# Values of both attentions projected with tokens on the partitions, 512 columns at a time, in two steps over K that hold four PSUM banks

## The chip, the cores and the metric

The kernel runs on one core of a Trainium2 chip (trn2). The metric is the device time of one execution in microseconds (us). The engines are named as the profile names them: PE (TensorE, with its weight loads PEld), DVE (VectorE), ACT (ScalarE), POOL (GpSimd) and SP (SyncE, which here issues the DMAs).

## What is computed

A trunk of two layers over 1024 tokens of width 1024, in float32. Only the mixer of the first layer is touched:

```
proj = rms_norm(x) @ w_in
gq, gk, gv, gr, glr, sq, sk, sv = split(proj, [256, 256, 512, 512, 16, 512, 512])
o_gla = gla_mixer(gq, gk, gv, gr, glr, ...)        # 4 heads, chunks of 64, decayed state
o_sb  = stick_breaking_mixer(sq, sk, sv, ...)      # 8 heads of 64, causal, no softmax
mix   = concat([o_gla, o_sb]) @ w_out
```

The mixer is followed by a SwiGLU block, a convolution layer and a second SwiGLU block, which the change leaves alone. The values are `gv` (512 columns of `w_in`, from column 512) and `sv` (512 columns, from column 2576).

## The kernel before

Every product of float32 matrices is made from three matmuls: both operands are split into a high and a low part (`split`, L88: ACT writes the high part, DVE the difference), and `mm3` (L211, matmuls at L213, L214 and L215) adds high by high, high by low and low by high in one PSUM bank. The normed input stands transposed in SBUF as `hT[h]`, one half h of 512 tokens each, features on the partitions (`hh_a`, `hl_a` in the trace).

A projection is made by `project2` (L435) for 256 columns of the weight and one half of the tokens: the weight columns are the stationary operand, the 512 tokens move, and each chunk of 128 columns fills one bank of the PSUM tag "a" (2 banks). The other tags are "b" (2 banks), "zw" (3) and "o" (1). Tiles of split weights come from a pool of 8 (`ws`), of which a `project2` step holds 4; raw weights have 2 buffers.

- `sb_v` (L577 to L586) uses `project2`, so its result stands with features on the partitions. ACT copies it out (`vt`), PE transposes it in four pieces into a bank of tag "b" (`vp`, L582), DVE copies that out (`vo`, L584), and a DMA stores it.
- `gla_v` makes the token layout directly: 128 tokens are stationary and 256 weight columns move, into half a bank of tag "a" (`pm_gv`), 24 matmuls for each of 4 token tiles, and ACT copies it out.
- `sb_q` also makes the sums of squares of a chunk on PE into a bank of tag "b" (`ms_q`, L556), which DVE reads in the first instruction of the inverse root (`nv_q`, L106).
- `gla_gate` (L469) makes the decay: `pm_glr`, then four single float32 matmuls `pg` (L484) into tag "a", each emptied by DVE and ACT (`lm`, `la`).

`run` takes a list of steps, hand-ordered at the end of the function. Each step's weights are fetched one step ahead. Steps of attention (`a0` for the first half of the tokens, `a1` for the second), of the decayed state (`g0`, `g1`) and of its output (`o0`, `o1`) are wrapped in `first`, which gives them a high priority: the scheduler places them as early as their inputs allow, and the projections that stand near them in the list fill PE between them. A unit of attention runs from PE (`z`) to ACT (sigmoid), DVE (a scan and a multiplication, `b`), PE (transposes `wt`), ACT and DVE (split into `wth`, `wtl`), PE (`po`) and back to ACT and DVE (`og`). The order on each engine is fixed when the program is built; each engine runs its list in order and waits on semaphores.

Of the kernel before, what the change touches and what calls it, by code (L numbers as in the profile page):

```python
# [8 lines left out]
F32 = mybir.dt.float32  # L9
F32R = mybir.dt.float32r  # L10
# [8 lines left out]
P = 128  # L19
D = 1024  # L20
T = 1024
NK = D // P
# [14 lines left out]
def r32(ap):  # L37
    return ap.bitcast(F32)
# [3 lines left out]
def trunk(ctx, tc, x, mix_norm, ffn_norm, hy_w_in, hy_w_gate2, hy_b_gate, hy_gla_norm,  # L42
          hy_sb_q_norm, hy_sb_k_norm, hy_w_out, cv_w_pw1, cv_b_pw1, cv_w_dw, cv_b_dw,
          cv_ln_g, cv_ln_b, cv_w_pw2, cv_b_pw2, ffn_w_gate, ffn_w_up, ffn_w_down, out):
    nc = tc.nc
# [8 lines left out]
    ident = const.tile([P, P], F32, name="ident")  # L54
# [33 lines left out]
    def split(hi, lo, src, scale=None, eng=None):  # L88
        if scale is None:
            nc.scalar.copy(hi, src)  # L90
            (eng or nc.vector).tensor_sub(lo, src, r32(hi))  # L91
        else:
            nc.scalar.mul(hi, src, scale)
            nc.vector.scalar_tensor_tensor(lo, src, scale, r32(hi), op0=ALU.mult, op1=ALU.subtract)
# [3 lines left out]
    raw_p = weights_es.enter_context(tc.tile_pool(name="raw", bufs=2))  # L98
    ws_p = weights_es.enter_context(tc.tile_pool(name="ws", bufs=8))
# [59 lines left out]
    def load_cols(w, c0, name, n=256):  # L159

        raw = raw_p.tile([P, NK, n], F32, name=f"raw_{name}", tag="raw")
        nc.sync.dma_start(raw, w[:, c0:c0 + n].rearrange("(k p) c -> p k c", p=P))
        return raw
# [7 lines left out]
    def parts(raw_ap, name, shape=(P, NK, P)):  # L171
        hi = ws_p.tile(list(shape), F32R, name=f"wh_{name}", tag="ws")
        lo = ws_p.tile(list(shape), F32R, name=f"wl_{name}", tag="ws")
        split(hi, lo, raw_ap, eng=weight_engine[0])
        return hi, lo
# [16 lines left out]
    def run(steps):  # L192
        ready = [s for s in steps if isinstance(s, tuple)]
        got = {}

        def fetch():
            if ready:
                s = ready.pop(0)
                got[id(s)] = s[0]()

        fetch()
        for s in steps:
            if isinstance(s, tuple):
                w = got.pop(id(s))
                fetch()
                s[1](w)
                marks.append(next(i for i in reversed(nc.cur_bb.bb.instructions) if i.engine == DVE))
            else:
                s()

    def mm3(ps, sh, sl, mh, ml, first, last, **kw):  # L211

        nc.tensor.matmul(ps, sh, mh, start=first, stop=False, **kw)  # L213
        nc.tensor.matmul(ps, sh, ml, start=False, stop=False, **kw)  # L214
        nc.tensor.matmul(ps, sl, mh, start=False, stop=last, **kw)  # L215
# [25 lines left out]
    def sub(i):  # L241
        return slice(P * (i % 4), P * (i % 4) + P)
# [88 lines left out]
    w_in = hy_w_in[0]  # L331
# [4 lines left out]
    gv_d = dr("gv_d", [T, 512])  # L336
    q_d = dr("q_d", [4, P, T])
    k_d = dr("k_d", [4, P, T])
    v_d = dr("v_d", [4, P, NT, P])
# [30 lines left out]
    with ExitStack() as es:  # L370
# [7 lines left out]
        class Ps:  # L378
            BUFS = {"a": 2, "b": 2, "zw": 3, "o": 1}

            def tile(self, shape, dt, name, tag):
                return psp.tile(shape, dt, name=name, tag=tag, bufs=self.BUFS[tag])

        ps = Ps()
        psum = lambda tag, name: ps.tile([P, 512], F32, name, tag)
        ft = lambda name: ftp.tile([P, 512], F32, name=name, tag="ft")
# [39 lines left out]
        hT = []  # L426
# [8 lines left out]
        def project2(c0, name, h, consume):  # L435

            def weights():
                raw = load_cols(w_in, c0, f"{name}{h}")
                return [parts(raw[:, :, P * c:P * c + P], f"{name}{h}{c}") for c in range(2)]

            def body(ws):
                for c, w in enumerate(ws):
                    pm = psum("a", f"pm_{name}_{c}{h}")
                    for k in range(NK):
                        mm3(pm, w[0][:, k, :], w[1][:, k, :], hT[h][0][:, k, :], hT[h][1][:, k, :],
                            k == 0, k == NK - 1)
                    consume(c, pm)

            return weights, body
# [62 lines left out]
                nc.sync.dma_start(gq_d[:, c, hsl(h)], s)  # L512
            return project2(0, "gq", h, consume)

        def gla_v(c, h):
            def weights():
                raw = load_cols(w_in, 512 + 256 * c, f"gv{c}{h}")
                return [parts(raw[:, 4 * kk:4 * kk + 4, :], f"gv{c}{h}{kk}", (P, 4, 256)) for kk in range(2)]

            def body(ws):  # L520
                for i in range(4 * h, 4 * h + 4):
                    pm = psum("a", f"pm_gv{c}{i}")[:, 0:256]
                    hh, hl = hT[i // 4]
                    for k in range(NK):
                        wh, wl = ws[k // 4]
                        mm3(pm, hh[:, k, sub(i)], hl[:, k, sub(i)], wh[:, k % 4, :], wl[:, k % 4, :],
                            k == 0, k == NK - 1)
                    vt = ft(f"gv_{c}{i}")[:, 0:256]
                    nc.scalar.copy(vt, pm)
                    nc.sync.dma_start(gv_d[P * i:P * i + P, 256 * c:256 * c + 256], vt)  # L530

            return weights, body

        def gate_r(r, h):
            def consume(c, pm):
# [26 lines left out]
        def sb_k(p2, h):  # L562
            def consume(c, pm):
                sq = ft(f"sq_k{p2}{c}{h}")
                nc.scalar.activation(sq, pm, AF.Square)
                y = ft(f"y_k{p2}{c}{h}")
                nc.vector.tensor_scalar_mul(y, pm, gk)
                ms = psum("b", f"ms_k{p2}{c}{h}")
                nc.tensor.matmul(ms, hones, sq, start=True, stop=True)
                act_in_set(sq, ms, AF.Ln, bias=eps_t)  # L570
                act_in_set(sq, sq, AF.Exp, scale=-0.5)
                nc.vector.tensor_mul(y, y, sq)
                nc.sync.dma_start(k_d[2 * p2 + c, :, hsl(h)], y)
            return project2(2064 + 256 * p2, f"k{p2}", h, consume)

        def sb_v(p2, h):
            def consume(c, pm):  # L577
                vt = ft(f"vt{p2}{c}{h}")
                nc.scalar.copy(vt, pm)
                pt = psum("b", f"vp{p2}{c}{h}")  # L580
                for i in range(4):
                    nc.tensor.transpose(pt[:, i * P:(i + 1) * P], vt[:, i * P:(i + 1) * P], ident)  # L582
                vo = ft(f"vo{p2}{c}{h}")
                nc.vector.tensor_copy(vo, pt)  # L584
                nc.sync.dma_start(v_d[2 * p2 + c, :, 4 * h:4 * h + 4, :], vo.rearrange("p (i d) -> p i d", i=4))
            return project2(2576 + 256 * p2, f"v{p2}", h, consume)  # L586


        def sb_units(h):
# [227 lines left out]
        def first(f):  # L817
            def run_first():
                with tc.high_priority(2000):
# [3 lines left out]
        a0, a1, g0, g1, o0, o1 = [[first(s) for s in f(h)] for f in (sb_steps, gla_steps, gla_out_steps)  # L823
                                  for h in range(2)]
        w0 = out_project(0, ps, lambda name: bcp.tile([P, T], F32, name=name, tag="bc")[:, 0:512])
# [3 lines left out]
        use_ln_exp = lambda: load_set(LN_EXP_SET)  # L829
        use_sigmoid = lambda: load_set(SIGMOID_SET)  # L830
        lx0, lxa = (lambda: load_x(0)), (lambda: xa.append(load_xa(1)))
        norm1 = lambda: input_norm(1, input_stats(1))
        q, k, v, gv, r = [[[f(p2, h) for h in range(2)] for p2 in range(2)]
                          for f in (sb_q, lambda p2, h: sb_k(p2, h), sb_v, gla_v, gate_r)]
        gkk, gqq = [[f(h) for h in range(2)] for f in (gla_k, gla_q)]
        q00 = q[0][0]

        def first_weights():
            with tc.issue_after(first_mul[0]), tc.issue_after(first_mul[1]):
# [1 line left out]

        q[0][0] = (first_weights, q00[1])
        first_mul = list(last_mul)
        run([q[0][0], lxa, load_columns, k[0][0], norm1, q[1][0], k[1][0], (gate_weights, gla_gate), v[0][0],
             use_sigmoid] + a0[:2] + [v[1][0]] + a0[2:4] + [gkk[0]] + a0[4:6] + [gqq[0]] + a0[6:8] + [gv[0][0]]
            + a0[8:10] + [gv[1][0]] + g0[:1] + a0[10:12] + [r[0][0]] + g0[1:2] + a0[12:14] + [r[1][0]] + g0[2:3]
            + a0[14:] + [q[0][1]] + g0[3:] + [v[0][1]] + o0[:2] + [q[1][1]] + o0[2:] + [v[1][1], gkk[1], lx0]
            + w0[0:1] + [gqq[1]] + w0[1:3] + [use_ln_exp, k[0][1], k[1][1], use_sigmoid] + w0[3:4] + [gv[0][1]]
            + w0[4:] + [gv[1][1], r[0][1], r[1][1]]
            + a1[:2] + [ffn_in] + interleave(f0[:-12], interleave(a1[2:], g1 + o1)) + f0[-12:])  # L850


# [184 lines left out]
    hT = {}  # L1037
# [4 lines left out]
    with ExitStack() as es:  # L1042
# [7 lines left out]
        ft = lambda name: ftp.tile([P, 512], F32, name=name, tag="ft")  # L1050
# [145 lines left out]
        c0 = conv_steps(0, range(NK))  # L1196
# [9 lines left out]
        blocks, _ = token_sums(1, hT["f10"], ps, ("n", "a"), ft, xn)  # L1206
        run(f10[14:16] + f10[17:])

    with ExitStack() as es:
        weight_engine[0] = nc.vector  # L1210
        steps, late = five_products(1, blocks, es, (("act", 6), ("s", 4), ("ft", 10)))
        store = lambda j: [nc.sync.dma_start(xout[i * P:(i + 1) * P, 512 * j:512 * j + 512],
                                             xres[i][:, 512 * j:512 * j + 512]) for i in range(NT)]
# [25 lines left out]
```

## Time and profile before

| | |
|---|---|
| median of 3 runs | 2274.56 us (2270.47 to 2276.02) |
| profiled execution | 2270.5 us, span 2268.7 us, granted clock 0.997 |
| PE busy | 2233.4 us, 98% of the span |
| DVE busy | 1579.7 us, 70% |
| ACT busy | 956.7 us, 42% |
| POOL busy | 493.9 us, 22% |
| bytes moved by DMA | 247.98 MB, mean 109 GB/s |

A matmul's busy time in the timeline covers its way through the array and overlaps its neighbours; what one costs is the distance between the starts of two that follow each other. One float32 matmul that isn't split leaves two records.

### The profile page before, as it was taken

Reading aid. Unit: us, or ns where it says so; the run is one execution under the profiler, and the core shown is the slowest. Engines: PE = TensorE matmul, PEld = TensorE weight load, DVE = VectorE, ACT = ScalarE, POOL = GpSimd, SP = SyncE. Lnnn points to the kernel's source line nnn. Section 1 sums busy time; section 2 is a strip of 40 time slices with the busy share of each in tenths; the row PEclk is TensorE's granted clock in tenths of the full one; section 3 lists DMA queues with packets and bytes.
Section 4 is the critical chain, followed back from the end, with each engine's and each line's share of the span. In section 5 each row is a group of like instructions: output and inputs, shape, how many; then the busy total and the mean of one; then the engine's idle time right before and its main releaser. Section 6 shows DMA issues by size and latency. Waiting matters only on the chain.

```text
span 2268.7 us, 28065 instructions
## 1 busy us (share of the span) xinstructions
PE 2233.4 (98%) x10602; PEld 1849.0 (82%) x10602; DVE 1579.7 (70%) x2647; ACT 956.7 (42%) x1594; POOL 493.9 (22%) x273
## 2 busy tenths in 40 slices
PE   7999999999999999999999999999999999999999
PEld 6788888888888887888888888788888788888887
DVE  6587764867788755466767744498844887787786
ACT  6465644755555433422222244466454322222221
POOL 0000000000000002544444444787744300000000
PEclk9999999999999999999999999999999999999999
DMA  6254554333342333232223322223432322232222
GB/s 207 97 155 147 183 177 134 105 90 100 128 123 77 119 120 136 77 110 93 93 80 106 112 84 93 93 93 125 134 104 84 110 90 84 66 111 85 65 89 93
DMA packets 221749, 247.98 MB, mean 109 GB/s; under 512 B 9733, under 2 KB 171632, under 8 KB 221614
## 3 DMA queue, kind: packets, MB, share of 16 engines
q1 hardware_dynamic: 221614, 246.19, 33.6%
q8 instruction: 83, 1.36, 0.2%
q14 instruction: 52, 0.43, 0.1%
HBM read 219.42 MB, written 26.74 MB: 108 GB/s over the span
## 4 chain that ended last, share of the span: by engine, by line
PE 91%; DVE 5%; ACT 2%; DMA 1%; issue 1%; SPq 0%; DVEq 0%; ACTq 0%
PE po L213 9%; PE po L214 9%; PE po L215 9%; PE pu L213 5%; PE pu L215 5%; PE pu L214 5%; PE pg L213 4%; PE pg L215 4%; PE pg L214 4%; PE pp L213 2%; PE pp L214 2%; PE pp L215 2%; PE po L684 2%; PE wt L666 1%; PE ps3u L213 1%; PE ps3u L214 1%
## 5 line engine op out<-in xcount | busy, mean ns | idle before, releaser
L1131 DVE SCALAR_TENSOR_TENSOR cs<-u,wd,cs 128x512 f32<-128x512 f32 x406 | 306.0, 754 | 11.1
L237 DVE TENSOR_TENSOR xr<-xr,po 128x512 f32<-128x512 f32 x232 | 158.5, 684 | 156.7 <-PE po L215 155.7
L91 POOL TENSOR_TENSOR wl_wo<-raw_wo,wh_wo 128x1024 fp32r<-128x1024 f32 x8 | 19.1, 2395 | 882.0 <-ACT wh_wo L90 882.0
L1026 DVE TENSOR_TENSOR xr<-xr,po 128x512 f32<-128x512 f32 x176 | 120.0, 683 | 100.6 <-PE po L215 100.5
L213 PE MATMUL pg<-hh_f,wh_g 128*128 128x512 f32 x440 | 173.4, 394 | 3.8 <-DVE s L285 3.6
L213 PE MATMUL po<-wh_d,a 128*128 128x512 f32 x440 | 173.5, 395 | 0.2
L214 PE MATMUL pg<-hl_f,wh_g 128*128 128x512 f32 x440 | 173.4, 394 | 0.0
L215 PE MATMUL pg<-hh_f,wl_g 128*128 128x512 f32 x440 | 173.0, 393 | 0.0
L214 PE MATMUL pu<-hl_f,wh_u 128*128 128x512 f32 x440 | 172.7, 393 | 0.0
L215 PE MATMUL pu<-hh_f,wl_u 128*128 128x512 f32 x440 | 172.4, 392 | 0.0
L213 PE MATMUL pu<-hh_f,wh_u 128*128 128x512 f32 x440 | 172.3, 392 | 0.0
L215 PE MATMUL po<-wh_d,a 128*128 128x512 f32 x440 | 171.9, 391 | 0.0
L214 PE MATMUL po<-wl_d,a 128*128 128x512 f32 x440 | 171.9, 391 | 0.0
L90 ACT CAST wh_g<-raw_g 128x1024 fp32r<-128x1024 f32 x55 | 58.0, 1054 | 167.7 <-PE po L214 100.2
L90 ACT CAST wh_d<-raw_d 128x1024 fp32r<-128x1024 f32 (+1 forms) x58 | 58.4, 1008 | 113.4 <-PE pu L214 62.2
L91 POOL TENSOR_TENSOR wl_g<-raw_g,wh_g 128x1024 fp32r<-128x1024 f32 x33 | 79.2, 2401 | 123.7 <-ACT wh_g L90 119.7
L213 PE MATMUL pp<-hh_c,wh_p 128*128 128x512 f32 x256 | 100.2, 395 | 3.4 <-ACT sg L1099 2.8
L213 PE MATMUL po<-wh_dp,ap 128*128 128x512 f32 x264 | 101.8, 391 | 1.6 <-ACT ap L90 0.8
L214 PE MATMUL po<-wl_dp,ap 128*128 128x512 f32 x264 | 101.3, 389 | 0.0
L214 PE MATMUL pp<-hl_c,wh_p 128*128 128x512 f32 x256 | 101.1, 395 | 0.0
L215 PE MATMUL po<-wh_dp,ap 128*128 128x512 f32 x264 | 101.0, 389 | 0.0
L215 PE MATMUL pp<-hh_c,wl_p 128*128 128x512 f32 x256 | 100.4, 393 | 0.0
(442 smaller groups left out, 6013.1 us busy)
## 6 DMA issues: line engine op xcount, KB each, us to landing
raw_g<-in_ffn_w_gate_dram SPq DMA_DIRECT2D x26, 1024.0 KB, 5.1
raw_u<-in_ffn_w_up_dram SPq DMA_DIRECT2D x26, 1024.0 KB, 5.2
raw_p<-in_cv_w_pw_dram SPq DMA_DIRECT2D x16, 1024.0 KB, 5.2
raw_d<-in_ffn_w_down_dram SPq DMA_DIRECT2D x26, 512.0 KB, 3.7
raw_g<-in_ffn_w_gate_dram SPq DMA_DIRECT2D x25, 512.0 KB, 4.9
raw_u<-in_ffn_w_up_dram SPq DMA_DIRECT2D x25, 512.0 KB
raw_dp<-in_ffn_w_down_dram SPq DMA_DIRECT2D x22, 512.0 KB
raw_d<-in_ffn_w_down_dram SPq DMA_DIRECT2D x10, 1024.0 KB, 4.9
```

The costliest lines, as they stand in the source:

```text
L90: nc.scalar.copy(hi, src)
L91: (eng or nc.vector).tensor_sub(lo, src, r32(hi))
L213: nc.tensor.matmul(ps, sh, mh, start=first, stop=False, **kw)
L214: nc.tensor.matmul(ps, sh, ml, start=False, stop=False, **kw)
L215: nc.tensor.matmul(ps, sl, mh, start=False, stop=last, **kw)
L237: nc.vector.tensor_add(xt[i][:, cs], xt[i][:, cs], po)
L666: nc.tensor.transpose(pt[:, col:col + P], wrow[bi][:, P * j:P * j + P], ident)
L684: nc.tensor.matmul(po[:, lo_c:256], st["v"][j // 4][:, j % 4, e, :], m[:, 256 * jj + lo_c:256 * jj + 256], start=(last and jj == 0 and m i ...
L1026: nc.vector.tensor_add(xres[i][:, cs], xres[i][:, cs], po)
L1131: i = nc.vector.scalar_tensor_tensor(out, tap, w, acc, op0=ALU.mult, op1=ALU.add)
```

## The change

`gla_v` and `sb_v` now share one function, `values`: the tokens are stationary in both, 512 weight columns move, and K is cut into two steps, each with its own weights. The four token tiles of a half keep four PSUM banks, both of tag "a" and both of tag "b", from the first step to the second. A step fetches two raw tiles of 512 KB and makes four tiles of split weights of 128x1024 in eight splits of 128x512 (before, four splits of 128x1024 a step). No transposes, `vt` layout or DVE copy remain for `sv`; its store writes four runs of 128 floats on each partition.

```diff
+        def values(c0, name, h, tile, store):
+            pm = {}
+            def weights(kk):
+                hi, lo = [[ws_p.tile([P, 2, 512], F32R, name=f"w{m}_{name}{h}{kk}{q}", tag="ws") for q in range(2)]
+                          for m in ("h", "l")]
+                for c in range(2):
+                    raw = raw_p.tile([P, 4, 256], F32, name=f"raw_{name}{c}{h}{kk}", tag="raw")
...
+                    for q in range(2):
+                        cs = slice(256 * c, 256 * c + 256)
+                        split(hi[q][:, :, cs], lo[q][:, :, cs], raw[:, 2 * q:2 * q + 2, :])
+            def body(kk, ws):
+                hh, hl = hT[h]
+                if kk == 0:
+                    for i in range(4):
+                        pm[i] = psum("ab"[i // 2], f"pm_{name}{i}{h}")
+                for i in range(4):
+                    for k in range(4 * kk, 4 * kk + 4):
+                        mm3(pm[i], hh[:, k, sub(i)], hl[:, k, sub(i)], ws[0][k % 4 // 2][:, k % 2, :],
+                            ws[1][k % 4 // 2][:, k % 2, :], k == 0, k == NK - 1)
+                    if kk == 1:
+                        vt = tile(f"{name}_{i}{h}")
+                        nc.scalar.copy(vt, pm[i])
+                        store(4 * h + i, vt)
-        def sb_v(p2, h):
-            def consume(c, pm):
-                vt = ft(f"vt{p2}{c}{h}")
-                nc.scalar.copy(vt, pm)
-                pt = psum("b", f"vp{p2}{c}{h}")
-                for i in range(4):
-                    nc.tensor.transpose(pt[:, i * P:(i + 1) * P], vt[:, i * P:(i + 1) * P], ident)
-                vo = ft(f"vo{p2}{c}{h}")
-                nc.vector.tensor_copy(vo, pt)
-                nc.sync.dma_start(v_d[2 * p2 + c, :, 4 * h:4 * h + 4, :], vo.rearrange("p (i d) -> p i d", i=4))
-            return project2(2576 + 256 * p2, f"v{p2}", h, consume)
+        def sb_v(h):
+            return values(2576, "v", h, ft, lambda i, vt: nc.sync.dma_start(
+                v_d[:, :, i, :].rearrange("c p d -> p c d"), vt.rearrange("p (c d) -> p c d", c=4)))
...
-        run([q[0][0], lxa, load_columns, k[0][0], norm1, q[1][0], k[1][0], (gate_weights, gla_gate), v[0][0],
-             use_sigmoid] + a0[:2] + [v[1][0]] + a0[2:4] + [gkk[0]] + a0[4:6] + [gqq[0]] + a0[6:8] + [gv[0][0]]
-            + a0[8:10] + [gv[1][0]] + g0[:1] + a0[10:12] + [r[0][0]] + g0[1:2] + a0[12:14] + [r[1][0]] + g0[2:3]
-            + a0[14:] + [q[0][1]] + g0[3:] + [v[0][1]] + o0[:2] + [q[1][1]] + o0[2:] + [v[1][1], gkk[1], lx0]
+        run([q[0][0], lxa, load_columns, k[0][0], norm1, q[1][0], k[1][0], (gate_weights, gla_gate)] + v[0]
+            + [use_sigmoid] + a0[:4] + [gkk[0]] + a0[4:6] + [gqq[0]] + a0[6:10] + gv[0]
+            + g0[:1] + a0[10:12] + [r[0][0]] + g0[1:2] + a0[12:14] + [r[1][0]] + g0[2:3]
+            + a0[14:] + [q[0][1]] + g0[3:] + o0[:2] + [q[1][1]] + o0[2:] + v[1] + [gkk[1], lx0]
```

In the order of PE before, at the gate, the four matmuls `pg` follow `pm_glr` and each other with nothing between (`pm_v0_00` is the first chunk of `sv`):

```order
L476 MATMUL pm_glr_1_787<-hh_a1_509,wg_681 128x512
L476 MATMUL pm_glr_1_787<-hl_a1_510,wg_681 128x512
L484 MATMUL pg_00_806<-glt0_785,w2_685 128x512
L484 MATMUL pg_01_819<-glt1_804,w2_685 128x512
L484 MATMUL pg_10_832<-glt0_785,w2_685 128x512
L484 MATMUL pg_11_845<-glt1_804,w2_685 128x512
L213 MATMUL pm_v0_00_868<-hh_a0_193,wh_v000_760 128x512
```

In the order of PE now, the same place: matmuls of `sv` stand between the `pg`, 19 behind the first, 6 behind the second (shown) and 11 behind the third.

```order
L484 MATMUL pg_01_825<-glt1_810,w2_685 128x512
L213 MATMUL pm_v30_883<-wh_v010_864,hh_a0_193 128x512
L214 MATMUL pm_v30_883<-wl_v010_866,hh_a0_193 128x512
L215 MATMUL pm_v30_883<-wh_v010_864,hl_a0_194 128x512
L214 MATMUL pm_v20_882<-wl_v011_867,hh_a0_193 128x512
L215 MATMUL pm_v20_882<-wh_v011_865,hl_a0_194 128x512
L213 MATMUL pm_v20_882<-wh_v011_865,hh_a0_193 128x512
L484 MATMUL pg_10_838<-glt0_791,w2_685 128x512
```

In the order of PE now, at the end of the first half's attention (`pgo30`, `pgo31`: the last tile of the decayed state, `pm_v21`: the third token tile of `sv` of the second half), no matmul of a projection stands in the 134 rows before `pm_v21`:

```order
L213 MATMUL pgo31_2600<-gsh3_2562,qz0_149 128x256
L214 MATMUL pgo31_2600<-gsl3_2563,qz0_149 128x256
L215 MATMUL pgo31_2600<-gsh3_2562,qz1_150 128x256
L213 MATMUL pm_v21_2873<-wh_v100_2673,hh_a1_509 128x512
L214 MATMUL pm_v21_2873<-wl_v100_2675,hh_a1_509 128x512
```

In the order of PE before, at the start of the same stretch (`z_300`: scores of a unit, `wt_211`: transposes of another), matmuls of `sv` of the second half stand between those of attention; further on it is those of `sq`, `sv` again, `gk` and `gq`, down to the last `pgo31`. These were some eight chunks of 24 matmuls each; now they stand before the stretch or behind it.

```order
L647 MATMUL z_300_1_0_2204<-maskr_112,identr_110 128x128
L649 MATMUL z_300_1_0_2204<-k1300_2188,qs300_2184 128x256
L213 MATMUL pm_v0_11_2770<-hh_a1_509,wh_v011_2553 128x512
L214 MATMUL pm_v0_11_2770<-hl_a1_510,wh_v011_2553 128x512
L215 MATMUL pm_v0_11_2770<-hh_a1_509,wl_v011_2554 128x512
L213 MATMUL pm_v0_11_2770<-hh_a1_509,wh_v011_2553 128x512
L214 MATMUL pm_v0_11_2770<-hl_a1_510,wh_v011_2553 128x512
L215 MATMUL pm_v0_11_2770<-hh_a1_509,wl_v011_2554 128x512
L666 MATMUL wt_211_2_2212<-ident_63,b_2112_2005 128x128
L666 MATMUL wt_211_2_2212<-ident_63,b_2113_2014 128x128 x2
L213 MATMUL pm_v0_11_2770<-hh_a1_509,wh_v011_2553 128x512
L214 MATMUL pm_v0_11_2770<-hl_a1_510,wh_v011_2553 128x512
```

In the order of DVE now, the read of `ms_q101`, which gives back the bank of tag "b" that `pm_v21` takes, stands behind all of that attention; the one of `ms_q111`, whose bank `pm_v31` takes, follows ten rows later. Before, the same two reads stood at the same place, but only `vp` waited for their banks.

```order
L113 TENSOR_TENSOR nt_g0_2617<-nt_g0_2617,nv_g0_2616 128x4
L113 TENSOR_TENSOR nt_g1_2649<-nt_g1_2649,nv_g1_2648 128x4
L114 SCALAR_TENSOR_TENSOR grs0_2615<-nt_g0_2617,grs0_2615 128x4
L106 TENSOR_SCALAR nv_q101_2724<-ms_q101_2719 128x8
L114 SCALAR_TENSOR_TENSOR grs1_2647<-nt_g1_2649,grs1_2647 128x4
L799 TENSOR_TENSOR on0_1807<-on0_1807,grs0_2615 128x512
```

## Rows read from the trace of the kernel before

**Rows 1.** The page, engines: busy time, share of the span, instructions.
```profile
PE 2233.4 (98%) x10602; PEld 1849.0 (82%) x10602; DVE 1579.7 (70%) x2647; ACT 956.7 (42%) x1594; POOL 493.9 (22%) x273
```

**Rows 2.** Windows: stretch, busy us of each engine, granted clock, DMA share, GB/s.
```profile
75.00:100.00 25.00, 23.81 (x81) 15.90 (x80) 17.93 (x23) 14.47 (x26) 0.00 (x0) 0.86 0.19 64
...
130.00:160.00 30.00, 29.15 (x196) 26.32 (x195) 24.54 (x44) 21.93 (x50) 0.00 (x0) 1.00 0.53 164
252.70:297.60 44.90, 44.90 (x240) 37.73 (x239) 32.53 (x83) 26.91 (x69) 0.00 (x0) 1.00 0.60 201
```

**Rows 3.** Timeline of PE, `gla_v` and output projection: start us, us, instruction.
```profile
365.82 0.28 PE L214 MATMUL pm_gv<-wl_gv,hh_a 128*128 128x256 f32 x1
...
368.82 0.28 PE L215 MATMUL pm_gv<-wh_gv,hl_a 128*128 128x256 f32 x1
...
371.01 0.39 PE L213 MATMUL po<-wh_wo,oTh 128*128 128x512 f32 x1
...
371.92 0.39 PE L214 MATMUL po<-wl_wo,oTh 128*128 128x512 f32 x1
```

**Rows 4.** Timeline of PE at a block of transposes of `sv`.
```profile
102.93 0.60 PE L582 MATMUL vp<-ident,vt 128*128 128x128 f32 x4
...
103.60 0.40 PE L214 MATMUL pm_v<-hl_a,wh_v 128*128 128x512 f32 x1
```

**Rows 5.** Timeline of PE at the gate; in brackets idle time before it and its releaser.
```profile
83.62 1.98 PE L484 MATMUL pg<-glt,w 32*128 32x512 f32 x4
86.31 3.31 PE L484 MATMUL pg<-glt,w 32*128 32x512 f32 x4 [0.71 <-DVE lm L491]
90.04 0.79 PE L213 MATMUL pm_v<-hh_a,wh_v 128*128 128x512 f32 x1 [0.43 <-DVE lm L491]
...
94.05 0.41 PE L213 MATMUL pm_v<-hh_a,wh_v 128*128 128x512 f32 x1
```

**Rows 6.** Timeline of PE at a float32 matmul that isn't split.
```profile
72.88 1.02 PE L569 MATMUL ms_k<-sq_k,hones 128*128 128x512 f32 x2
...
73.97 0.40 PE L213 MATMUL pm_k<-hh_a,wh_k 128*128 128x512 f32 x1
```

**Rows 7.** Timeline of PE after its longest wait for DVE.
```profile
455.35 0.50 PE L213 MATMUL pg<-hh_f,wh_g 128*128 128x512 f32 x1 [3.60 <-DVE s L285]
...
455.95 0.63 PE L215 MATMUL pg<-hh_f,wl_g 128*128 128x512 f32 x1
...
459.33 0.39 PE L214 MATMUL pg<-hl_f,wh_g 128*128 128x512 f32 x1
```

**Rows 8.** Groups of DVE by form, 100 to 345 us: busy us, mean ns | idle before.
```profile
L764 DVE SCALAR_TENSOR_TENSOR S<-S,dec,pu 64x128 f32<-64x128 f32 x32 | 11.1, 347 | 4.8 <-PE pu L215 4.1
L654 DVE TENSOR_TENSOR_SCAN b<-b 128x512 f32<-128x512 f32 x8 | 9.8, 1222 | 1.6 <-ACT b L320 1.6
...
L91 DVE TENSOR_TENSOR wtl<-wt,wth 128x256 fp32r<-128x256 f32 x16 | 6.6, 410 | 0.2 <-ACT wth L90 0.2
...
L91 DVE TENSOR_TENSOR wtl<-wt,wth 128x512 fp32r<-128x512 f32 x8 | 5.5, 687 | 0.5 <-ACT wth L90 0.4
...
L91 DVE TENSOR_TENSOR wtl<-wt,wth 128x128 fp32r<-128x128 f32 x16 | 4.5, 281 | 0.7 <-ACT wth L90 0.7
...
L654 DVE TENSOR_TENSOR_SCAN b<-b 128x128 f32<-128x128 f32 x8 | 3.4, 422 | 1.0 <-ACT b L320 1.0
...
L113 DVE TENSOR_TENSOR nt_g<-nt_g,nv_g 128x4 f32<-128x4 f32 x12 | 1.5, 158 | 0.0
```

**Rows 9.** Timeline of DVE, a scan and what follows it.
```profile
244.42 1.23 DVE L654 TENSOR_TENSOR_SCAN b<-b 128x512 f32<-128x512 f32 x1 [0.41 <-ACT b L320]
245.56 0.40 DVE L91 TENSOR_TENSOR wtl<-wt,wth 128x256 fp32r<-128x256 f32 x1
```

**Rows 10.** Timeline of PE, transposes of attention and what follows them.
```profile
204.07 0.60 PE L666 MATMUL wt<-ident,b 128*128 128x128 f32 x4
204.42 0.48 PE L214 MATMUL pm_r<-hl_a,wh_r 128*128 128x512 f32 x1
```

More of the change, by code (lines that the diff above doesn't have):

```diff
@@ L513, in gla_q @@
             return project2(0, "gq", h, consume)
[L515 to L528, printed above, removed]
-                    nc.scalar.copy(vt, pm)
-                    nc.sync.dma_start(gv_d[P * i:P * i + P, 256 * c:256 * c + 256], vt)
-            return weights, body
+        def values(c0, name, h, tile, store):
[5 more added lines that the diff above has]
+                    raw = raw_p.tile([P, 4, 256], F32, name=f"raw_{name}{c}{h}{kk}", tag="raw")
+                    r0, cc = 4 * P * kk, c0 + 256 * c
+                    nc.sync.dma_start(raw, w_in[r0:r0 + 4 * P, cc:cc + 256].rearrange("(k p) c -> p k c", p=P))
+                    for q in range(2):
+                        cs = slice(256 * c, 256 * c + 256)
+                        split(hi[q][:, :, cs], lo[q][:, :, cs], raw[:, 2 * q:2 * q + 2, :])
+                return hi, lo
+            def body(kk, ws):
[11 more added lines that the diff above has]
+                        store(4 * h + i, vt)
+            return [(lambda kk=kk: weights(kk), lambda ws, kk=kk: body(kk, ws)) for kk in range(2)]
@@ L534, in gate_r, with gla_v @@
+        def gla_v(h):
+            return values(512, "gv", h, ft, lambda i, vt: nc.sync.dma_start(gv_d[P * i:P * i + P, :], vt))
         def gate_r(r, h):
@@ L574, in sb_k @@
             return project2(2064 + 256 * p2, f"k{p2}", h, consume)
-        def sb_v(p2, h):
-            def consume(c, pm):
-                vt = ft(f"vt{p2}{c}{h}")
-                nc.scalar.copy(vt, pm)
-                pt = psum("b", f"vp{p2}{c}{h}")
-                for i in range(4):
-                    nc.tensor.transpose(pt[:, i * P:(i + 1) * P], vt[:, i * P:(i + 1) * P], ident)
-                vo = ft(f"vo{p2}{c}{h}")
-                nc.vector.tensor_copy(vo, pt)
-                nc.sync.dma_start(v_d[2 * p2 + c, :, 4 * h:4 * h + 4, :], vo.rearrange("p (i d) -> p i d", i=4))
-            return project2(2576 + 256 * p2, f"v{p2}", h, consume)
+        def sb_v(h):
+            return values(2576, "v", h, ft, lambda i, vt: nc.sync.dma_start(
+                v_d[:, :, i, :].rearrange("c p d -> p c d"), vt.rearrange("p (c d) -> p c d", c=4)))
         def sb_units(h):
@@ L832, in trunk @@
         norm1 = lambda: input_norm(1, input_stats(1))
-        q, k, v, gv, r = [[[f(p2, h) for h in range(2)] for p2 in range(2)]
-                          for f in (sb_q, lambda p2, h: sb_k(p2, h), sb_v, gla_v, gate_r)]
+        q, k, r = [[[f(p2, h) for h in range(2)] for p2 in range(2)] for f in (sb_q, sb_k, gate_r)]
+        v, gv = [[f(h) for h in range(2)] for f in (sb_v, gla_v)]
         gkk, gqq = [[f(h) for h in range(2)] for f in (gla_k, gla_q)]
@@ L843, in trunk @@
         first_mul = list(last_mul)
-        run([q[0][0], lxa, load_columns, k[0][0], norm1, q[1][0], k[1][0], (gate_weights, gla_gate), v[0][0],
-             use_sigmoid] + a0[:2] + [v[1][0]] + a0[2:4] + [gkk[0]] + a0[4:6] + [gqq[0]] + a0[6:8] + [gv[0][0]]
-            + a0[8:10] + [gv[1][0]] + g0[:1] + a0[10:12] + [r[0][0]] + g0[1:2] + a0[12:14] + [r[1][0]] + g0[2:3]
-            + a0[14:] + [q[0][1]] + g0[3:] + [v[0][1]] + o0[:2] + [q[1][1]] + o0[2:] + [v[1][1], gkk[1], lx0]
-            + w0[0:1] + [gqq[1]] + w0[1:3] + [use_ln_exp, k[0][1], k[1][1], use_sigmoid] + w0[3:4] + [gv[0][1]]
-            + w0[4:] + [gv[1][1], r[0][1], r[1][1]]
+        run([q[0][0], lxa, load_columns, k[0][0], norm1, q[1][0], k[1][0], (gate_weights, gla_gate)] + v[0]
+            + [use_sigmoid] + a0[:4] + [gkk[0]] + a0[4:6] + [gqq[0]] + a0[6:10] + gv[0]
+            + g0[:1] + a0[10:12] + [r[0][0]] + g0[1:2] + a0[12:14] + [r[1][0]] + g0[2:3]
+            + a0[14:] + [q[0][1]] + g0[3:] + o0[:2] + [q[1][1]] + o0[2:] + v[1] + [gkk[1], lx0]
+            + w0[0:1] + [gqq[1]] + w0[1:3] + [use_ln_exp, k[0][1], k[1][1], use_sigmoid] + w0[3:]
+            + gv[1] + [r[0][1], r[1][1]]
             + a1[:2] + [ffn_in] + interleave(f0[:-12], interleave(a1[2:], g1 + o1)) + f0[-12:])
```

## The prediction

> **What bounds the kernel now.** I read the page's engine rows first: PE is busy 98% of the span, DVE 70%, ACT 42% [rows 1]. PE is the bound, so the change can only gain by taking PE work or PE idle time away, and can only lose by making PE wait. The windows by stage come second. In the second half of the first attention, 252.7 to 297.6 us, PE is busy 44.90 of 44.90 us, and DVE 32.53 of them [rows 2]. Attention itself does not fill PE there: projections stand between its instructions (the order in the section on the change), and they hide how long DVE takes. Between 75 and 100 us the granted clock is 0.86 [rows 2], the one weak place that the change touches. Last I read the timelines of what is edited [rows 3 to 7] and DVE's prices [rows 8, 9].
>
> **The change part by part.**
>
> *`gv` with 512 columns.* Before, 25 matmuls of 256 columns take 368.82 − 365.82 = 3.00 us, 0.120 each; four of 512 take 371.92 − 371.01 = 0.91, 0.2275 each [rows 3]. There are 2 column chunks x 8 token tiles x 24 = 384 of the first, and now 8 x 24 = 192 of the second: 46.1 − 43.7 = **2.4 us gained**. The Trainium skill (TensorE: Matmul & The Clock Gate, section Back-to-back issue gap) gives a lone matmul its columns' time plus 2.5 ns; by that, an estimate from the page, the 192 matmuls saved would be worth 0.5 us and the sum would be 1.9 us later; the rows have the duration, so I use theirs.
>
> *No transposes of `sv`.* From the start of a block of four to the second matmul behind it are 0.67 us, of which one matmul is 0.23: 0.44 a block [rows 4], eight blocks: **3.5 us gained**. The matmuls of `sv` moved 512 columns before as well, so their number and length stay.
>
> *The gate.* Four `pg` run from 83.62 to 90.04, 6.42 us, with waits for DVE between them [rows 5]. One float32 matmul of 512 columns costs 73.97 − 72.88 − 0.23 = 0.86 [rows 6], four of them 3.4, so 3.0 us are idle. Behind them nine matmuls take 4.01 us instead of 9 x 0.2275 = 2.05 [rows 5]: PE had idled and ran at the lower of its two levels, 1.2 instead of 2.4 GHz (0.86 is the window's mean [rows 2]). That is another 1.9. Now 19, 6 and 11 matmuls of `sv` stand in the three gaps, 36 x 0.2275 = 8.2 us of work for 3.0 us of idleness. I take all of it: **4.9 us gained**; at worst nothing.
>
> So 2.4 + 3.5 + 4.9 = **10.8 us gained**.
>
> *The four banks held.* `values` takes both banks of tags "a" and "b". For the second half's `sv`, `pm_v21` and `pm_v31` need the banks of `ms_q101` and `ms_q111`, which DVE frees by `nv_q`. Those reads have no priority and stand in DVE's list behind all the rest of the first half's attention. PE runs its list in order, so `pm_v21` waits, and behind it everything on PE. The next projection, `gk`, cannot be put ahead either: the two steps of `sv` hold all eight tiles of split weights until they have run. Hence the 134 rows of PE without a projection. What they last is set by DVE. From `wtl_211_2`, which needs a transpose at the head of that stretch of PE, to the read of `ms_q101` stand 88 DVE instructions:
>
> - 18 of 256 columns at 0.410: 7.4; 11 of 512 at 0.687: 7.6; 5 of 128 at 0.281: 1.4
> - 8 scans of 128 to 512, two of each size, mean of 0.422 and 1.222: 6.6
> - 16 updates of S at 0.347: 5.6; 22 tiny ones at 0.158: 3.5
> - 8 multiplications of 127 to 511, half way between 0.281 and 0.687: 3.9
>
> Together 36.0 us [rows 8]. The work of PE beside them is 50 transposes and small matmuls at 0.35/4 = 0.088 [rows 10], 73 of 256 columns at 0.120 and 8 larger ones at up to 0.2275 [rows 3]: 14.9 us. How tightly DVE can pack its 36.0 us the trace of before doesn't show, as PE was always the slower one. The bounds: instructions that follow each other directly overlap by 244.42 + 1.23 − 245.56 = 0.09 us [rows 9], so never under 36.0 − 88 x 0.09 = 28.1. At the densest DVE of any attention window, 24.54 of 30.00, it is 44.0; at the share of this very stretch, 32.53 of 44.90, it is 49.7 [rows 2]. So PE idles 13, 29 or 35 us. I take **29 us lost**: each product passes PE, ACT and DVE several times, which keeps DVE from its floor, but without projections in between PE answers sooner than in the last of these windows.
>
> The Trainium skill (Perfetto Trace Analysis, section Matmuls) says that independent groups should rotate through different PSUM banks, so that one is emptied while the next runs. It speaks against holding four. By the rows of before alone, where PE never idles at an eviction in the last window, this would cost 0; by that rule it would cost the term just made.
>
> *The clock after it.* After its longest wait for DVE, 3.60 us, PE needs 3.38 us for eight matmuls that take 1.8 at full clock [rows 7]; the gate showed 1.9 lost [rows 5]. A longer idle stretch ends the same way: **1.8 us lost**.
>
> *At nothing.* Splits of 512 columns cost DVE 2 x 0.687 for what took one of 1024; eight copies of `vo` on DVE go. Both lie beside a PE that is 98% busy, and ACT has 58% left [rows 1]. The stores of `sv` are cut in shorter runs and the raw weights come in two loads a step; the DMA share is 0.53 to 0.60 there [rows 2], and none of it is waited for unless a step's load follows a late split; that is in the upper end below. The attention starts 66 rows of PE later, so its fillers are used up earlier: the same loss seen from the other side, not a further one.
>
> **The sum.** −10.8 + 29 + 1.8 = +20.0 us. The profiled execution was 2270.5 us, so 2290.5; it lies 4.1 below the median of the runs, and on the median it is 2274.56 + 20.0 = **2294.5 us**. About 0.3% (6.8 us) is what a measurement of this kernel can tell from no change.
>
> **Rivals.**
>
> 1. *The stretch stays hidden: faster.* If DVE gets through those 88 instructions in the 14.9 us that PE needs, only the gains stay: 2274.56 − 10.8 = 2263.8. It decides below 14.9 + 4 us of DVE time, where the gain still exceeds 0.3%. For it: today's window has no idle PE. Against it: that window has projections in it, and the floor of 28.1. It needs DVE prices about half of those in the rows. Chance 0.07.
> 2. *DVE packs to its floor.* Without PE in its way DVE runs nearly back to back: 13 us idle, net +4, 2278.6; up to 18 idle, 2284. For it: DVE has several units in flight. Against it: DVE waits for ACT in nearly every group [rows 8]. Chance 0.15, of which 0.06 lies within 0.3%.
> 3. *The chain itself is the pace.* Loads of a unit wait for earlier stores on the one DMA queue, and DVE's share stays at 72% or falls: 35 us idle, net +26, 2300.6; with a few waits for loads 2308. Chance 0.13.
> 4. *Something else takes half back*, such as earlier work on DVE that lets it run ahead: within 0.3%. Chance 0.06.
>
> The forecast, 18 to 35 us idle and 2284 to 2300, has 0.59.
>
> **How the numbers follow.** Faster: rival 1, 0.07. Within 0.3%: 0.06 + 0.06 = 0.12. Slower: 0.59 + 0.09 + 0.13 = 0.81. The range of 8 in 10 leaves out rival 1, the lower part of rival 4 and the far tail of rival 3: 2275 to 2307; its ends are the packed floor and the 72% pace with some waits.
>
> **What would show it.** Right: PE has one wait of several us for DVE at `pm_v21`, released by an instruction of `nv_q`, and many short ones before it from some 235 to 290 us, with PE busy a third to a half of that window and a granted clock under 1; the `pg` follow without a gap near 83 us; no `vp`; 192 `pm_gv` of 512 columns. Wrong: PE as busy as now in that window (rival 1), or the reads of `ms_q101` early. If the wait comes for a weight split or a load instead of `nv_q`, the cause that I give is wrong even if the time is right.

## The result, and the profile after

The changed kernel takes 2291.40 us (median of 4 runs, 2288.91 to 2295.76), the kernel before 2274.99 us (4 runs, 2270.47 to 2276.02): ratio 1.0077, 95% interval 1.0065 to 1.0089. That is 16.4 us slower, where 20.0 were forecast. The profiled execution of the changed kernel took 2293.3 us, 22.8 more than that of before. What follows compares these two, the fastest run of the kernel before and the second slowest of the changed one, so its sum is that of this pair and not of the medians.

The page of the changed kernel, engines, beside [rows 1]:

```profile
PE 2237.4 (98%) x10378; PEld 1843.2 (80%) x10378; DVE 1577.6 (69%) x2655; ACT 959.1 (42%) x1602; POOL 492.5 (21%) x273
```

PE has 224 instructions fewer: 192 matmuls of `gv` and 32 transposes of `sv`. Its busy time is not shorter, since matmuls at the lower clock last longer and count as busy. The share of the span says nothing here; the windows do (columns as in [rows 2]):

```profile
75.00:100.00 25.00, 25.00 (x95) 16.99 (x94) 14.41 (x21) 11.64 (x21) 0.00 (x0) 1.00 0.31 106
...
130.00:160.00 30.00, 27.30 (x134) 21.43 (x133) 22.45 (x38) 20.78 (x45) 0.00 (x0) 1.00 0.67 207
...
235.00:250.00 15.00, 12.70 (x69) 10.19 (x67) 6.57 (x17) 5.12 (x12) 0.00 (x0) 1.00 0.78 244
250.00:265.00 15.00, 9.84 (x48) 8.00 (x48) 12.43 (x27) 8.61 (x21) 0.00 (x0) 0.68 0.23 55
265.00:280.00 15.00, 10.55 (x46) 9.21 (x47) 10.38 (x21) 11.29 (x25) 0.00 (x0) 0.63 0.76 259
280.00:295.00 15.00, 8.10 (x37) 6.09 (x36) 10.36 (x35) 8.16 (x33) 0.00 (x0) 0.59 0.24 67
295.00:310.00 15.00, 15.00 (x67) 12.52 (x67) 13.59 (x78) 7.23 (x22) 0.00 (x0) 0.84 0.36 107
```

At the gate the window is full and the clock 1.00 instead of 0.86. From 130 to 160 us, in the first units of attention, PE idles 2.7 us where it idled 0.85 [rows 2]. From 250 to 295 us, where PE was busy all the time before, it is busy 28.5 of 45 us at a granted clock of 0.59 to 0.68: this is the stretch without projections.

The timeline of PE through it, with the idle time before an instruction and its releaser in brackets (`pgo` at 247.42 is the last of tile 1, `pm_v` at 296.45 is `pm_v21`):

```profile
247.42 0.28 PE L215 MATMUL pgo<-gsh,qz 128*128 128x256 f32 x1
250.51 0.33 PE L653 MATMUL z<-k,qs 128*128 128x128 f32 x1 [2.81 <-ACT k L90]
...
266.25 0.80 PE L213 MATMUL pgo<-gsh,qz 128*128 128x256 f32 x2 [3.50 <-ACT gsh L90]
...
293.27 0.80 PE L213 MATMUL pgo<-gsh,qz 128*128 128x256 f32 x2 [4.59 <-DVE nv_g L109]
...
296.45 0.77 PE L213 MATMUL pm_v<-wh_v,hh_a 128*128 128x512 f32 x1
...
299.94 0.40 PE L215 MATMUL pm_v<-wh_v,hl_a 128*128 128x512 f32 x1
```

The timeline of DVE, the first and the last of the instructions that the prediction counted (`wtl_211_2` and the read of `ms_q101`), and then the window between them:

```profile
251.99 0.42 DVE L91 TENSOR_TENSOR wtl<-wt,wth 128x256 fp32r<-128x256 f32 x1
...
296.20 0.17 DVE L106 TENSOR_SCALAR nv_q<-ms_q 128x8 f32<-128x8 f32 x1
```

```profile
251.99:296.20 44.21, 28.45 (x125) 23.45 (x126) 32.90 (x89) 27.69 (x80) 0.00 (x0) 0.62 0.39 124
```

From one to the other are 44.2 us; 44.0 were forecast. `pm_v21` itself hardly waits: the last of PE's own attention instructions starts at 296.24, just as the bank comes free. The waits are spread over the attention, 18.6 us in all from 250 us on in waits of over 0.2 us, the 2.81 ahead of the counted stretch among them. Instructions of ACT ended 11.8 of these us, instructions of DVE 6.8. The rest of the loss goes with the lower clock on what little PE has to do.

The timeline of PE at the gate:

```profile
85.30 1.12 PE L484 MATMUL pg<-glt,w 32*128 32x512 f32 x2
86.35 0.50 PE L213 MATMUL pm_v<-wh_v,hh_a 128*128 128x512 f32 x1
86.69 0.40 PE L214 MATMUL pm_v<-wl_v,hh_a 128*128 128x512 f32 x1
...
98.67 0.40 PE L214 MATMUL pm_v<-wl_v,hh_a 128*128 128x512 f32 x1
```

From 85.30 to 98.67 stand four `pg` and 37 matmuls of `sv`: 13.37 − 37 x 0.2275 = 4.95 us for what took 8.4 with its idle time and its slow clock [rows 5].

### The profile page after: what moved, and what is told of

The parts are those of the page before. It is cut to its first block, busy times and chain, and to the rows that moved or that the text cites. A ratio compares the mean times of both kernels' runs of the same rounds, so it can differ in the third digit from the quotient of the medians.

```text
span 2291.3 us, 27651 instructions
## 1 busy us (share of the span) xinstructions
PE 2237.4 (98%) x10378; PEld 1843.2 (80%) x10378; DVE 1577.6 (69%) x2655; ACT 959.1 (42%) x1602; POOL 492.5 (21%) x273
## 4 chain that ended last, share of the span: by engine, by line
PE 90%; DVE 5%; DMA 2%; ACT 2%; issue 1%; SPq 0%; DVEq 0%; ACTq 0%
PE po L213 9%; PE po L214 9%; PE po L215 9%; PE pu L213 5%; PE pu L215 4%; PE pu L214 4%; PE pg L213 4%; PE pg L215 4%; PE pg L214 4%; PE pp L213 2%; PE pp L214 2%; PE pp L215 2%; PE po L692 2%; PE wt L674 1%; PE ps3u L213 1%
```

## The experiments

Three theories of the lost 30 us were told apart. **A, the banks:** `values` needs banks of tag "b" that `ms_q` gives back late, so the scheduler puts no projection into the end of the attention. **B, the weight tiles:** the two steps of `values` hold all eight tiles of split weights, and that keeps projections out. **C, the order of the list:** the projections are spent earlier and none is left, whatever the banks do. In the order of the changed kernel the inverse root of `sq` waits for its scratch tiles, `nv` and `nt`, of which there are two each, shared with the inverse roots of the decayed state's output (`gla_out`), and two of these stand ahead of it in the list and run at the very end of the attention.

**Scratch tiles of their own for `sq`.**

```diff
-        v = small.tile([P, n], F32, name=f"nv_{name}", tag="nv")
-        t = small.tile([P, n], F32, name=f"nt_{name}", tag="nt")
+        v = small.tile([P, n], F32, name=f"nv_{name}", tag="nvq" if name[0] == "q" else "nv")
+        t = small.tile([P, n], F32, name=f"nt_{name}", tag="ntq" if name[0] == "q" else "nt")
```

> The changed kernel, with scratch buffers of their own (two each) for the inverse roots of sq, which so far shared two with the inverse roots of the decayed state's output. Theory A (banks): the read of ms_q101 waits for those buffers, so its bank of tag b comes late and the third value tile with it. With own buffers the read stands 97 rows earlier in DVE's order and projections fill PE up to the last two pairs of units; from there to the end of the attention two stretches of 29 and 30 rows with no projection are left, about half of the 44 us that DVE needed, with 12 us of PE work in them: some 10 us idle instead of 29. About 2272 us (2267 to 2277), and no PE wait of over 1 us before 265 us. Rival B (weight tiles): the eight tiles of split weights are what keeps projections out; then PE waits at pm_gk for its weights and the time stays at 2287 to 2293. Rival C (fillers spent earlier, wherever they stand): 2285 or more.

Measured: 2312.17 us, ratio to before 1.0179 (1.0162 to 1.0196): 20 us slower than the change instead of 20 faster. The same edit in the kernel before:

> The kernel before with the same scratch buffers of their own for the inverse roots of sq, and nothing else. In it the banks of ms_q held up only transposes vp, which PE has other work for. Theory A: no difference, 2270 to 2277. If the scratch buffers were worth something by themselves, whatever the values do, it would be faster by 5 us or more.

Measured: 2305.50 us, 1.0144 (1.0129 to 1.0159). No theory had that. In the kernel before, the loss lies in no one place: from 400 us on, the matmuls that took 100 us now take 0.9 to 2.5 us longer in all but one of these stretches, in the feed-forward blocks as well, where nothing was edited. The edit also adds 128 bytes of scratch in front of the weights, so that all weight buffers start 128 bytes further. The kernel before with 128 bytes that nothing reads, and with 512:

```diff
+    nc.vector.memset(small.tile([P, 16], F32, name="pad", tag="pad"), 0.0)
```

> The kernel before with a scratch tile of 64 bytes a partition in two buffers that nothing reads (one more memset): the order on every engine is that of before, and all buffers behind it, weights and weight splits among them, lie 128 bytes further in SBUF. If where the buffers lie made the kernel with own scratch buffers 33 us slower, this one is at 2298 to 2310, with gate and up matmuls 0.232 to 0.234 apart instead of 0.225 to 0.230. If the scratch buffers cost it by their waits or orders, this one is at 2270 to 2277.

Measured: 2303.11 us, 1.0128 (1.0111 to 1.0146). The groups of PE between 1000 and 1300 us with 128 bytes of padding (busy us and mean ns of one behind the bar):

```profile
L214 PE MATMUL pg<-hh_f,wh_g 128*128 128x512 f32 x138 | 54.5, 395 | 0.0
...
L215 PE MATMUL pg<-hl_f,wh_g 128*128 128x512 f32 x137 | 54.1, 395 | 0.0
```

> The kernel before with the same unread scratch tile made 512 bytes in all, so that weights and everything else behind it lie 512 instead of 128 bytes further. If the loss at 128 bytes comes from where a buffer starts within 512 bytes, this one is at 2270 to 2277 with matmuls 0.2275 us apart. If any move costs it, 2298 or more.

Measured: 2272.21 us, 1.0001 (0.9991 to 1.0010). The same groups with 512 bytes:

```profile
L214 PE MATMUL pg<-hh_f,wh_g 128*128 128x512 f32 x144 | 56.0, 389 | 0.0
L215 PE MATMUL pg<-hl_f,wh_g 128*128 128x512 f32 x144 | 56.0, 389 | 0.0
```

So it is where the buffers start that costs 28 of these 33 us, 6 ns on a matmul of the feed-forward blocks. In the changed kernel these matmuls take 389 ns as before, so this is no part of what the change costs.

The first run's time says nothing of theory A, but its trace does. With nothing changed but the scratch tiles, the read of `ms_q101` comes at 230.91 instead of 296.20 us, and between 235 and 345 us PE idles 9.8 us instead of 18.8 (the windows of the changed kernel and then of this one):

```profile
230.91 0.17 DVE L106 TENSOR_SCALAR nv_q<-ms_q 128x8 f32<-128x8 f32 x1 [0.55 <-PE ms_q L572]
```

```profile
235.00:345.00 110.00, 91.19 (x419) 75.05 (x418) 69.53 (x195) 52.12 (x124) 0.00 (x0) 0.83 0.55 171
```

```profile
235.00:345.00 110.00, 100.19 (x488) 80.62 (x487) 72.87 (x188) 51.47 (x126) 0.00 (x0) 0.95 0.56 173
```

A run that joins these scratch tiles with `gv` moved early (the diff of "More projections late" below) was expected at 2261 to 2270 us and took 2309.47, ratio 1.0158 (1.0143 to 1.0173). It has the same moved buffers, so its time says as little; PE idles 3.0 us between 235 and 345 us in it. The next run gets the early read without a byte moved.

**The root of `sq` ahead in the list.**

```diff
-            + a0[14:] + [q[0][1]] + g0[3:] + o0[:2] + [q[1][1]] + o0[2:] + v[1] + [gkk[1], lx0]
+            + a0[14:] + [q[0][1]] + g0[3:] + [q[1][1]] + o0 + v[1] + [gkk[1], lx0]
```

> The changed kernel with one step moved in the list: the last projection of sq of the second half ahead of the first two outputs of the decayed state, so that its inverse roots get the two shared scratch buffers first. Nothing is added and no buffer moves; the order on the engines is that of the kernel with own scratch buffers (read of ms_q101 97 rows of DVE earlier, two stretches of 29 and 30 rows of PE without a projection instead of one of 134). Theory A (the bank of tag b comes late because its reader waits for scratch): 2271 to 2279, most of the loss gone, from that kernel's PE idle time less what its own extra cost in all stretches was. If own scratch buffers cost 30 us through these orders and not through where buffers lie in memory, this one is at 2300 or more as well. Rival B (weight tiles) or C (fillers spent early): 2286 to 2293.

Measured: 2279.28 us, 1.0019 (1.0009 to 1.0029): some 12 us faster than the change, just above what was expected. The reads of `ms_q101` and `ms_q111` in DVE's timeline, the first at 230.59 instead of 296.20 us, and then the windows of this kernel:

```profile
230.59 0.17 DVE L106 TENSOR_SCALAR nv_q<-ms_q 128x8 f32<-128x8 f32 x1 [0.73 <-PE ms_q L572]
...
239.40 0.17 DVE L106 TENSOR_SCALAR nv_q<-ms_q 128x8 f32<-128x8 f32 x1 [0.40 <-PE ms_q L572]
```

```profile
265.00:280.00 15.00, 15.00 (x75) 11.84 (x75) 8.74 (x17) 4.72 (x10) 0.00 (x0) 1.00 0.33 104
280.00:295.00 15.00, 13.20 (x68) 10.90 (x66) 8.29 (x15) 8.00 (x17) 0.00 (x0) 1.00 0.88 291
295.00:310.00 15.00, 12.52 (x48) 9.93 (x49) 10.57 (x20) 9.93 (x22) 0.00 (x0) 0.66 0.58 173
310.00:325.00 15.00, 9.94 (x53) 8.01 (x52) 11.97 (x56) 8.69 (x42) 0.00 (x0) 0.77 0.49 150
```

PE stays full to 280 us. What is left is a gap of 9.3 us of idleness in the last 45 us of the attention, where the projections have run out: that part is theory C's, as the run with `gv` moved as well bears out further on. B by itself is out, since these steps hold all eight weight tiles as they did.

**Two banks instead of four.** Each token tile is finished over all of K in a rotating bank of tag "a", with the same weights held.

```diff
-                    for k in range(4 * kk, 4 * kk + 4):
-                        mm3(pm[i], hh[:, k, sub(i)], hl[:, k, sub(i)], ws[0][k % 4 // 2][:, k % 2, :],
...
+                pm[kk] = ws
+                if kk == 0:
+                    return
+                for i in range(4):
+                    po = psum("a", f"pm_{name}{i}{h}")
+                    for k in range(NK):
+                        hi, lo = pm[k // 4]
```

> The changed kernel, but each token tile of the values is finished in one go over all of K, in a bank of tag a that rotates, so that no bank of tag b and no more than two banks are held; the eight tiles of split weights are held as before, and the shared scratch buffers stay. Theory A: values no longer wait for the bank of ms_q101; one stretch of 55 rows without a projection is left at the end of the attention. About 2274 us (2268 to 2282). Rival B: all eight weight tiles are still held, so nothing is gained, 2287 to 2293, with waits for weights in PE's rows.

Measured: 2282.17 us, 1.0039 (1.0024 to 1.0054): half of the loss is gone with all eight weight tiles held, which speaks against B once more. It stands just above the upper end of the expectation. One reason was not thought of: without matmuls of a first step, the gate, worth 3.4 us, has its gap back. PE's timeline there:

```profile
85.90 2.82 PE L484 MATMUL pg<-glt,w 32*128 32x512 f32 x4 [0.73 <-DVE lm L491]
89.62 0.80 PE L213 MATMUL pm_v<-wh_v,hh_a 128*128 128x512 f32 x1 [0.90 <-DVE lm L491]
```

**More projections late, with the bank late.** `gv` of the second half is moved ahead in the list of the change, the root of `sq` is not.

```diff
-            + w0[0:1] + [gqq[1]] + w0[1:3] + [use_ln_exp, k[0][1], k[1][1], use_sigmoid] + w0[3:]
-            + gv[1] + [r[0][1], r[1][1]]
+            + w0[0:1] + [gqq[1]] + gv[1] + w0[1:3] + [use_ln_exp, k[0][1], k[1][1], use_sigmoid] + w0[3:]
+            + [r[0][1], r[1][1]]
```

> The changed kernel with gv of the second half moved ahead as in the last one, but the bank of ms_q101 as late as in the change: PE's order keeps its 134 rows without a projection, since the step put there needs the same banks. Theory A: no gain, 2286 to 2295. Rival C (too few projections left that late): the steps moved up fill the stretch, 2280 or less.

Measured: 2300.18 us, 1.0115 (1.0098 to 1.0131): no gain, and 9 us worse, more than either theory said. Its windows show the same gap as the change:

```profile
250.00:265.00 15.00, 9.85 (x48) 7.99 (x48) 12.39 (x27) 8.97 (x22) 0.00 (x0) 0.68 0.18 49
...
280.00:295.00 15.00, 8.64 (x37) 6.72 (x37) 10.31 (x35) 8.03 (x33) 0.00 (x0) 0.50 0.26 72
```

C alone does not make the gap: projections that were moved to it do not enter while the bank is held. Part of the 9 us is at the feed-forward block, which now lacks `gv` in front of it: PE waits 2.8 us for `sr` there, and idles 4.4 us between 420 and 560 us instead of 0.6.

**Both: the root ahead and `gv` early** (the last two diffs together).

> The same, and gv of the second half ahead of the output projection's second step: the longest stretch of PE without a projection is 18 rows, as before the change. Theory A: 2267 to 2277; PE not idle for more than 1 us at once between 235 and 300 us. By where the buffers lie this is the kernel before, so matmuls of the feed-forward blocks are 0.2275 us apart again.

Measured: 2273.35 us (10 runs), 0.9996 (0.9986 to 1.0005). Two windows of it:

```profile
280.00:295.00 15.00, 15.00 (x77) 12.72 (x76) 8.06 (x17) 9.32 (x21) 0.00 (x0) 1.00 0.98 299
295.00:310.00 15.00, 15.00 (x80) 12.58 (x79) 10.78 (x17) 9.86 (x18) 0.00 (x0) 1.00 0.59 214
```

The gap is closed, at full clock. The time is that of the kernel before all the same. Between 60 and 560 us PE idles 10.9 us, where it idled 6.8 in the kernel before (the windows of the kernel before and then of this one):

```profile
60.00:560.00 500.00, 493.23 (x2636) 414.41 (x2635) 352.49 (x653) 276.07 (x540) 0.00 (x0) 0.99 0.42 133
```

```profile
60.00:560.00 500.00, 489.06 (x2409) 400.76 (x2408) 348.92 (x658) 277.42 (x544) 0.00 (x0) 0.99 0.43 136
```

So some 4 of the 9 us of gains go into idle time; where the rest went was not traced. The new waits are spread (1.5 us at `ms_k`, 1.4 at the output projection). The largest stands where projections now are missing, at the feed-forward block, behind the gates r that DVE empties; it takes the place of the 3.60 us that the kernel before lost at that block [rows 7] and that the change had got rid of. In PE's timeline:

```profile
428.62 0.79 PE L213 MATMUL pu<-hh_f,wh_u 128*128 128x512 f32 x1 [2.82 <-DVE sr L554]
```

**The gates r early instead**, all of them and then half of them, with the root ahead.

```diff
-            + w0[0:1] + [gqq[1]] + w0[1:3] + [use_ln_exp, k[0][1], k[1][1], use_sigmoid] + w0[3:]
-            + gv[1] + [r[0][1], r[1][1]]
+            + w0[0:1] + [gqq[1], r[0][1], r[1][1]] + w0[1:3] + [use_ln_exp, k[0][1], k[1][1], use_sigmoid] + w0[3:]
+            + gv[1]
```

> The changed kernel with the last projection of sq ahead of the outputs of the decayed state (as in the run with that one step moved), and the gates r of the second half, not gv, ahead of the output projection's second step. The longest stretch of PE without a projection is 18 rows, and gv, whose banks ACT empties, stands last before the feed-forward block, where the gates r kept DVE and with it PE waiting for 4 us and a slow clock. Theory A: 2261 to 2270, faster than the kernel before by about 7 us: the gains of 9.3 us less some 2 us of waits at sk and the output projection. If the values in four banks cost something by themselves, or if the wait at the feed-forward block stays, 2271 to 2277.

Measured: 2270.26 us (11 runs), 0.9994 (0.9985 to 1.0003), between its two cases. The wait for `sr` is gone, but with only `gv` in front of it the feed-forward block now waits for its norm:

```profile
430.07 1.11 PE L155 MATMUL pt_f<-ident,xn_f 128*128 128x128 f32 x4 [2.15 <-DVE hl_f L94]
```

```diff
+            + w0[0:1] + [gqq[1], r[0][1]] + w0[1:3] + [use_ln_exp, k[0][1], k[1][1], use_sigmoid] + w0[3:]
+            + gv[1] + [r[1][1]]
```

> As the last one, but only the first two chunks of the gates r go ahead of the output projection's second step; the other two stay behind gv. One stretch of 30 rows without a projection is left at the end of the first attention (3 to 6 us of idle PE), and 33 instead of 22 us of projections stand before the feed-forward block, where both-early left PE waiting 6 us for the norm. Theory A, with projections as a cover that is moved from one gap to the other: 2264 to 2271, the better of the two by a few us if the block's gap closes to the 0.6 us that it had with all of r behind. If the two gaps just trade one for one: 2268 to 2274.

Measured: 2285.37 us, 1.0056 (1.0041 to 1.0070), outside both cases. It has both gaps, 9.3 us idle between 300 and 340 us and the wait of 3.6 us at the feed-forward block, and a wait of 3.5 us for `xr` in a later block, of which more below. No version beats the kernel before by more than a measurement can tell.

## Why the prediction was right

Its forecast (slower, 2294.5 us, range 2275 to 2307) held, and its main term was met almost exactly, in part by luck. Step by step:

- *`gv` at 512 columns, 2.4 us:* right. The new matmuls are as far apart as forecast, 1.13 us for five in PE's timeline:

```profile
410.56 0.39 PE L214 MATMUL pm_gv<-wl_gv,hh_a 128*128 128x512 f32 x1
...
411.69 0.84 PE L213 MATMUL pm_gv<-wh_gv,hh_a 128*128 128x512 f32 x3
```

- *No transposes, 3.5 us:* they are gone; what they cost can't be seen apart from the rest.
- *The gate, 4.9 us:* mis-sized; 8.4 − 4.95 = 3.4 us. The idle time and the slow clock did go, but there was less idle time than the 3.0 us of the sum: the brackets of [rows 5] show 0.71 + 0.43. A lone `pg` between matmuls of `sv` costs 1.24 us (4.95 / 4) and not the 0.86 of the row that it was priced by [rows 6]: that row is another float32 matmul of as many columns, on all 128 rows of the array, where `pg` uses 32; whether that is the reason was not tried.
- *The stretch, 29 us:* right in size, 44.2 − 14.9 = 29.3 (14.9 is the prediction's own figure for PE's work). The bank was the cause as far as it went: freeing it took half of the idle time out, and most of the rest went when projections were moved there as well. Three things were wrong in the account. The reads of `ms_q` come late because two scratch tiles are shared: with their own, and no more priority than before, they come at 230.91. The sign that was named for being right, a wait of several us at `pm_v21` that an instruction of `nv_q` ends, did not come: the order that the late bank imposes had PE wait within the attention. And DVE did not set the length of the stretch alone: PE waited longer for ACT (11.8 us) than for DVE (6.8).
- *How long the stretch lasts, 44.0 us:* met at 44.2 by two errors that cancelled. The prices of the 88 instructions held, but 36.0 adds their durations one by one and so counts their overlaps twice, while the share of 24.54 / 30.00 that it was divided by counts them once. DVE was busy 32.9 us, at a share of 0.74, close to the 0.72 that this stretch had before and not the 0.82 that was taken. 32.9 us at 0.82 would have been 40.2.
- *The clock after it, 1.8 us:* right; eight matmuls from 296.45 to 299.94 take 3.49 us instead of 1.82.
- *Not in the sum:* the wait of 2.8 us for `k` just ahead of the stretch; a new one of 1.7 us at `ms_k` (the waits of PE, below); and a gain, the wait of 3.6 us for DVE at the feed-forward block [rows 7] shrank to 0.5 and took its slow clock with it, some 4.7 us.

```profile
PE ms_k L585 <- ACT sq_k L581: 1.7, 1, 1.7
...
PE pg L213 <- DVE s L285: 0.5, 1, 0.5
```

Together −2.4 − 3.5 − 3.4 + 29.3 + 1.7 + 2.8 + 1.7 − 4.7 = +21.5, beside 22.6 between the two spans. That is closer than the terms are good for: the sum leaves out 1.9 us more of idle time between 130 and 160 us, and a wait of 3.5 us for `xr` in a later block that the profile of before doesn't have. With both it would be 26.9, so the terms are good to some 4 us. The causes of these two were not looked for, but the wait for `xr` is not the change's own: five of the thirteen profiles have it, among them that of the kernel before with scratch tiles of its own. It is in the 22.8 us between the two profiled executions; that the medians lie only 16.4 apart is otherwise in the spread of the runs, 5.6 and 6.9 us in the two kernels.

The floor (13 us idle) and the ceiling (35) were far apart, and the choice between them was not shown by the trace of before. The rule of the Trainium skill (Perfetto Trace Analysis, section Matmuls) that independent groups should rotate through different PSUM banks fits the time here: two rotating banks instead of four held ones gave half of the loss back, at 2282.17 us. Its reason, that one bank is emptied while the next group runs, is not what these runs show: in the stretch PE had no wait for a copy of the values, and the bank was late because of a reader of what stood in it before.

Rival 1 (the stretch stays hidden) fell, and the last experiments show that its price was wrong too: with the stretch hidden the time is that of the kernel before (0.9996 and 0.9994) and not 10.8 us less. A projection that fills one gap is missing at another, which accounts for some 4 of these us.

## What to carry to other kernels

Before a step is given more PSUM banks, look at who must give them back and what that reader itself waits for; here a scratch tile of 32 bytes held a bank, and giving it back early took half of PE's idle time out of the stretch (18.8 to 9.8 us). Where the bound engine is kept full by independent work, count that work like a budget: whatever is spent earlier, or shut out, opens a gap elsewhere, and the order of the built program shows it before any run. A change that adds or drops a buffer has moved all buffers behind it, so compare it with a kernel in which only the place moves.

## What the runs showed of the hardware

Where buffers start in SBUF is worth more than the whole change: 128 bytes of unread padding cost the kernel before 28 us (1.0128), a mean matmul of the feed-forward blocks going from 389 to 395 ns, and 512 bytes cost nothing (1.0001). Which of the buffers behind it must start at such a place was not tried. A float32 matmul on 32 rows among split ones cost 1.24 us, more than the 0.86 of one on 128 rows.
